# Score products on all 128 rows, and the delta rule's 64-row products taken in turn from both halves

## The chip, the cores and the metric

The kernel runs on one core of a Trainium2 chip. The metric is the device time of one execution, in microseconds (us); lower is better. The core's engines work beside each other, each through its own queue in order: TensorE (PE in the profile; PEld is its loading of stationary operands), VectorE (DVE), ScalarE (ACT), GpSimd (POOL) and the sync engine (SP), which issues the DMAs.

## The reference, cut to what matters

Four layers over one sequence of 512 positions with width 1024, in float32: an even layer (a gated recurrence and gated linear attention), an odd layer (attention with a decay), and two hybrid layers, each followed by a dense block. The change touches three things. In the odd layer, 16 heads of 64 columns:

```
s = q @ k.T                       # 512 x 512 for each head, by blocks of 128 queries
s = s + f_cum[t] - f_cum[s]       # decay, then the causal mask
o = softmax(s) @ v
```

In a hybrid layer, the same kind of scores for 4 heads with a window of 128 keys (two heads share keys) and for 4 heads with two sets of keys each, and a gated delta rule for 4 heads of 128 columns, in 8 chunks of 64 positions:

```
v_new = u_c - w_c @ state
o_c   = qd_c @ state + qk_c @ v_new
state = state * gl_c + kd_c.T @ v_new
```

## The kernel before

**Precision.** A float32 operand is split in two parts: a high part, rounded to a shorter float32 form (fp32r in the profile), and a low part, which is the rest. A projection's tile is the sum of three products in one accumulator (`mm3`, lines 590 to 592). `nc.tensor.matmul` loads its stationary operand (`lhsT`) and streams the moving one (`rhs`); each call issues its own load. Products on plain float32 operands (the transposes, the delta rule) take two passes for a call.

**Scores.** `scores` (line 1333) makes one block of 128 queries for one head. `stack` (line 1354) puts the high part of a head's 64 rows of q on one half of a 128-row tile and the low part on the other half. For k, the high part stands on both halves, so that the first product (line 1340, 128 rows) adds high by high and low by high; the second (line 1341, 64 rows of the half that holds q's high part) adds high by low. A product is at least 256 columns wide. Then VectorE adds the mask and takes the maximum (line 1349) and ScalarE the exponential (line 1351). `weigh` transposes the block (line 1371), `values` multiplies it with v (line 1385: 128 rows, 64 columns of the array, heads in turn on the two halves of the columns). `attend` (line 1388) runs these as three steps: at step t, the scores of unit t, the transposes of unit t - 3, the values of unit t - 5. Projections, gates and output products are called between units at listed steps.

In `fox` (the odd layer), `prepare` splits the operands of a pair of heads: four copies of k's high part on ScalarE (line 1503) and two low parts on GpSimd (line 1504), and two stacked q's; it is called at the fifth of the eight units of the pair before (`PREP`). The units of 8 pairs make 64 scores. `first_half`, at the eight steps of `FOX_O`, runs one tile of the first half of the output product each (`out_steps`, whose `add_gated` multiplies by a gate on VectorE, line 700, and adds to x on GpSimd, line 701); at the first of them `fetch_x` issues all eight loads of x on the sync queue. In `hybrid`, `prep_a` does the splitting for the windowed heads (low parts on VectorE, line 1717), `pair_a` and `pair_b` make 16 and 32 scores; `pair_b`'s keys stand on both halves in high and low part already.

**Delta rule.** `gdn_head` (line 1997) is a generator of about 30 steps; `skew` runs four of them, each 12 steps behind the one before, with projections called between. Its chunks lie by twos in a 128-row tile: an even chunk on rows 0 to 63, an odd one on 64 to 127. `invert16` solves 16-row blocks by many small VectorE steps and holds two accumulators meanwhile. Then lines 2118 to 2124 make a 128x128 matrix for each of six chunks: a 64-row product and a VectorE combination in turn, in the order 1, 3, 5, 2, 4, 6. The scan (lines 2126 to 2133) does, per chunk, a 64-row product (line 2129) and, on its sum, a 128-row product with the state before (line 2131), and copies the state out (line 2132). Last, lines 2135 to 2140 make the output: a 128-row product for each tile of two chunks, each followed by its two 64-column products with the states.

**Order.** The scheduler of the tile framework keeps each engine's queue about in the program's order, and lets later instructions pass those that it expects to wait. There are eight accumulators (one bank each): three for projections (`psm`), five for all else (`ps`). Work tiles are 43 slots, handed out first in, first out (`_Slots`); a slot's new user waits for its last.

Of the kernel before, what the change touches and what calls it, by code (L numbers as in the profile page):

```python
# [12 lines left out]
F32 = mybir.dt.float32  # L13
# [315 lines left out]
class _Kernel:  # L329
# [682 lines left out]
    def keep_x(self, i):  # L1012

        for h, (c, n) in enumerate(HALVES):
            self.nc.sync.dma_start(self.xkeep[i, :, c:c + n], self.x[i][h])

    def fetch_x(self, src=None, scale=None):
        src = self.xkeep if src is None else src
        for i in range(NT):
            self.x[i] = self.f(2)  # L1020
            for h, (c, n) in enumerate(HALVES):
                self.nc.sync.dma_start(self.x[i][h], src(i)[:, c:c + n] if callable(src) else src[i, :, c:c + n])
                if scale is not None:
                    (self.nc.gpsimd.tensor_scalar(self.x[i][h], self.x[i][h], scale, None, op0=OP.mult) if FXS else self.nc.scalar.activation(self.x[i][h], self.x[i][h], AF.Copy, scale=scale))
# [308 lines left out]
    def scores(self, q, k, n, bias, scale, first=None):  # L1333


        nc = self.nc
        ps = self.ps()
        if isinstance(q, tuple):
            w = max(n, 256)
            nc.tensor.matmul(ps[:, :w], lhsT=q[0], rhs=k[0], start=True, stop=False)  # L1340
            nc.tensor.matmul(ps[:, :w], lhsT=q[1], rhs=k[1], start=False, stop=True)  # L1341
        else:
            nc.tensor.matmul(ps[:, :n], lhsT=q, rhs=k, start=True, stop=True)
        s = self.f()
# [9 lines left out]
    def stack(self, t, b, at, eng):  # L1354

        d = self.slots.take(R32)
        src, hi, lo = t[b:b + 64], d[at:at + 64], d[64 - at:128 - at]
        self.nc.scalar.activation(hi, src, AF.Copy)
        eng.tensor_tensor(lo, src, hi.bitcast(F32), op=OP.subtract)
        return d  # L1360

    def scale(self, s, n, r):
# [56 lines left out]
    def fox(self, gate, done):  # L1419
# [71 lines left out]
        def pair(p):  # L1491
# [3 lines left out]
            def prepare():  # L1495
                q, k = qT.pop(p), kT.pop(p)
                st["q"] = [self.stack(q, hh * 64, hh * 64, nc.gpsimd) for hh in range(2)]
                st["k"] = [self.slots.take(R32) for _ in range(2)]
                lo = st["l"] = self.slots.take(R32)
                for hh, d in enumerate(st["k"]):  # L1500
                    b = slice(hh * 64, hh * 64 + 64)
                    for o in (hh * 64, 64 - hh * 64):
                        nc.scalar.activation(d[o:o + 64], k[b], AF.Copy)
                    nc.gpsimd.tensor_tensor(lo[b], k[b], d[b].bitcast(F32), op=OP.subtract)
                self.free(q, k)
# [12 lines left out]
            def score(i, hh):  # L1518
                def f():
# [4 lines left out]
                    n = i * 128 + 128  # L1524
                    b = slice(hh * 64, hh * 64 + 64)
                    fb, fd = st[hh]
# [3 lines left out]
                    w = max(n, 256)  # L1530
                    q, k, lo = st["q"][hh], st["k"][hh], st["l"]
                    s, m, l, r = self.scores((q[:, SL[i]], q[b, SL[i]]), (k[:, :w], lo[b, :w]), n, bias, 1.0)
                    v.reciprocal(r, l)
                    self.scale(s, n, r)
                    if i == NT - 1:
                        self.free(fb, fd)
                        if hh:
                            self.free(st["q"], st["k"], st["l"])
                    return s
# [27 lines left out]
        def first_half(t):  # L1567
            if not off:
                self.fetch_x()
                off.append(self.out_steps("od_out", 0, 0, 4, lambda k: mix[k], gate))  # L1570
            next(off[0])
            if t == FOX_O[-1]:
# [32 lines left out]
    def hybrid(self, l, gate, done):  # L1605
# [99 lines left out]
        def prep_a(p):  # L1705
            b = p * 64
            if not p:
                for h in range(2):
                    d = self.slots.take(R32)
                    ka.append(d)  # L1710
                    for o in (64 * h, 64 - 64 * h):
                        nc.scalar.activation(d[o:o + 64], ak[h * 64:h * 64 + 64], AF.Copy)
                d = self.slots.take(R32)
                ka.append(d)
                for h in range(2):
                    q = slice(h * 64, h * 64 + 64)
                    (nc.gpsimd, v)[STK[3]].tensor_tensor(d[q], ak[q], ka[h][q].bitcast(F32), op=OP.subtract)
                self.free(ak)
# [14 lines left out]
        def pair_a(p):  # L1733
            st = {}

            def score(i, hh):
                def f():
                    if i == 0 and hh == 0:
                        st["o"] = self.ps()
                    b = slice(p * 64, p * 64 + 64)  # L1740
                    j0 = max(0, i - 1)
                    n = (i + 1 - j0) * 128
                    x = p * 8 + i * 2 + hh
                    c = slice(j0 * 128, j0 * 128 + 256)
                    q = qa[p][hh]
                    s, m, ll, r = self.scores((q[:, SL[i]], q[b, SL[i]]), (ka[p][:, c], ka[2][b, c]), n, [(slice(0, n), band[:, 256 - n:])], 0.125, nsink[:, x:x + 1])
                    nc.scalar.activation(r, m, AF.Exp, bias=smt[:, 32 + x:33 + x])
# [3 lines left out]
                    if i == NT - 1 and hh:  # L1751
                        self.free(qa[p], ka[p], ka[2] if p else ())
                    return s
# [15 lines left out]
        def pair_b(p):  # L1769
            st = {}  # L1770

            def score(i, g, hh):
                def f():
                    if i == 0 and g == 1 and hh == 0:
                        st["o"] = self.ps()
                    n = i * 128 + 128
                    b = slice(hh * 64, hh * 64 + 64)
                    w = max(n, 256)
                    q, (kh, kl) = qb[p][hh], kb[g - 1]
                    s, m, ll, r = self.scores((q[:, SL[i]], q[b, SL[i]]), (kh[:, :w], kl[b, :w]), n, [(slice(0, n), cm[:, 512 - n:])], 0.125)  # L1780
                    v.reciprocal(r, ll)
# [215 lines left out]
    def gdn_head(self, h, g, xs, outs):  # L1997
# [119 lines left out]
        yield  # L2117
        for n in (1, 3, 5, 2, 4, 6):
            i, c0 = n // 2, (n % 2) * 64
            if n < 3:  # L2120
                ps = self.ps()
            q = ps[:, SL[(n - 1) // 2]]
            mm(q, lhsT=tw[c0:c0 + 64, SL[i]], rhs=kd[c0:c0 + 64, SL[i]], start=True, stop=True)  # L2123
            v.scalar_tensor_tensor(mt[n], self.ident, gl[:, n:n + 1], q, op0=OP.mult, op1=OP.subtract)
        yield
        for n in range(7):
            i, c0 = n // 2, (n % 2) * 64
            ps = self.ps()
            mm(ps[:, :128], lhsT=kd[c0:c0 + 64, SL[i]], rhs=tu[c0:c0 + 64, SL[i]], start=True, stop=n == 0)  # L2129
            if n:  # L2130
                mm(ps[:, :128], lhsT=mt[n], rhs=ss[n - 1], start=False, stop=True)
            v.tensor_copy(ss[n], ps[:, :128])
            yield
        po = self.ps()
        for i in range(NT):
            mm(po[:, SL[i]], lhsT=dt[:, SL[i]], rhs=tu[:, SL[i]], start=True, stop=False, skip_group_check=True)
            for n in (2 * i, 2 * i + 1):
                if n:
                    c0 = (n % 2) * 64
                    mm(po[c0:c0 + 64, SL[i]], lhsT=qd[:, n * 64:n * 64 + 64], rhs=ss[n - 1], start=False, stop=True, skip_group_check=True)  # L2140
        yield
# [106 lines left out]
```

## Time and profile before

| | us |
|---|---|
| Median of 3 runs | 2871.63 (2868.56 to 2872.33) |
| The profiled execution | 2869.14 |
| its span, first to last instruction | 2867.4 |
| PE busy | 2766.4 (96%) |
| DVE busy | 1972.8 (69%) |
| ACT busy | 1143.1 (40%) |
| POOL busy | 673.8 (23%) |

Engines work beside each other, so their busy times don't add up to the span. The lines of the scores have their first and last records between 720 and 2461 us; the odd layer's attention lies at about 715 to 985 us, the delta-rule stages at 1435 to 1580 and 2190 to 2340, the hybrid attentions behind each, to 1730 and 2490. The chain of waits follows back, from the last instruction, what released each step or what stood before it on its engine; the time that it shows for a product is what that product adds to the chain, which is less than its duration, since products overlap. "x4" behind a piece counts the passes merged in it.

### The profile page before, as it was taken

To read this page: it belongs to the slowest core of one execution; us is meant where nothing else is said; L and a number is where in the kernel's file an instruction comes from. 1 tells how busy PE (TensorE), PEld (TensorE's weight loads), DVE (VectorE), ACT (ScalarE), POOL (GpSimd) and SP (SyncE) were. 2 spreads that over 40 slices of the span, in tenths; PEclk is the share of its full clock that TensorE was granted. 3 is DMA by queue.
4 is the path that set the end of the run, shared out by engine and by line. 5 is a ranking of instruction groups with operands and counts; after the bars stand their busy time and mean duration, and the time that the engine had idled before them with its cause. 6 is when DMAs were issued, how large, how long until landed. Compare 5 with 4: busy or idle time off the path is not lost.

```text
span 2867.4 us, 38053 instructions
## 1 busy us (share of the span) xinstructions
PE 2766.4 (96%) x13780; PEld 2193.2 (76%) x13780; DVE 1972.8 (69%) x4170; ACT 1143.1 (40%) x2195; POOL 673.8 (23%) x530
## 2 busy tenths in 40 slices
PE   7999999998999989999999999999999999999998
PEld 5768788876666868887887668888888766788887
DVE  8978756665557776667888777666579878764445
ACT  3825233353555523324433444223254235433221
POOL 1042522435324262224011211100300112101112
PEclk9999999999999999999999999999999999999999
DMA  8635455422112355552222314554332131243322
GB/s 293 213 108 184 160 179 179 153 96 96 45 55 78 97 182 191 198 184 95 96 66 62 109 36 153 180 190 177 133 110 76 52 109 46 74 142 108 96 94 76
DMA packets 114332, 356.22 MB, mean 124 GB/s; under 512 B 13520, under 2 KB 14560, under 8 KB 114144
## 3 DMA queue, kind: packets, MB, share of 16 engines
q1 hardware_dynamic: 114144, 353.80, 36.9%
q8 instruction: 108, 1.77, 0.3%
q14 instruction: 80, 0.66, 0.1%
HBM read 341.16 MB, written 8.39 MB: 122 GB/s over the span
## 4 chain that ended last, share of the span: by engine, by line
PE 74%; DVE 8%; issue 2%; ACT 2%; POOL 1%; DMA 1%; DVEq 0%; SPq 0%; POOLq 0%; ACTq 0%
PE mm L590 20%; PE mm L591 20%; PE mm L592 20%; PE w L1385 2%; DVE wlo L597 2%; PE w L1371 2%; PE w L1341 2%; PE w L1340 1%; PE w L1009 1%; DMA adaw<-in_ada_r_dram 1%; ACT whi L596 1%; PE w L2129 1%; DVE f L762 1%; PE w L2105 1%; PE w L2123 1%
## 5 line engine op out<-in xcount | busy, mean ns | idle before, releaser
L596 ACT ACTIVATE whi<-raw 128x512 fp32r<-128x512 f32 (+1 forms) x798 | 488.4, 624 | 933.6 <-PE mm L591 436.0
L597 DVE TENSOR_TENSOR wlo<-raw,whi 128x512 fp32r<-128x512 f32 (+1 forms) x764 | 587.1, 789 | 239.9 <-ACT whi L596 225.6
L590 PE MATMUL mm<-uh,whi 128*128 128x512 f32 (+2 forms) x1896 | 720.3, 380 | 8.5 <-ACT uh L596 3.8
L591 PE MATMUL mm<-ul,whi 128*128 128x512 f32 (+2 forms) x1896 | 716.0, 378 | 1.0 <-DVE ul L597 0.7
L592 PE MATMUL mm<-uh,wlo 128*128 128x512 f32 (+2 forms) x1896 | 715.0, 377 | 0.0
L590 PE MATMUL mm<-whi,f 128*128 128x512 f32 x1120 | 449.7, 402 | 3.1 <-ACT f L596 3.1
L591 PE MATMUL mm<-wlo,f 128*128 128x512 f32 x1120 | 445.2, 398 | 0.7 <-DVE wlo L597 0.7
L592 PE MATMUL mm<-whi,f 128*128 128x512 f32 x1120 | 445.4, 398 | 0.5 <-DVE f L597 0.5
L590 PEld LDWEIGHTS mm<-uh,whi 128*128 128x128 f32 (+1 forms) x1896 | 357.6, 189 | 78.9 <-ACT uh L596 5.0
L591 PEld LDWEIGHTS mm<-ul,whi 128*128 128x128 f32 (+1 forms) x1896 | 357.2, 188 | 69.3 <-issue 3.3
L592 PEld LDWEIGHTS mm<-uh,wlo 128*128 128x128 f32 (+1 forms) x1896 | 357.4, 188 | 67.4 <-issue 2.3
L701 POOL TENSOR_TENSOR f<-f,f 128x512 f32<-128x512 f32 x144 | 203.2, 1414 | 860.3 <-DVE f L700 795.9
L590 PEld LDWEIGHTS mm<-whi,f 128*128 128x128 f32 x1120 | 212.0, 189 | 56.9 <-issue 4.9
L592 PEld LDWEIGHTS mm<-whi,f 128*128 128x128 f32 x1120 | 211.5, 189 | 52.6 <-issue 2.1
L591 PEld LDWEIGHTS mm<-wlo,f 128*128 128x128 f32 x1120 | 211.7, 189 | 50.3 <-issue 1.7
L700 DVE TENSOR_TENSOR f<-mm,gate 128x512 f32<-128x512 f32 x144 | 98.6, 686 | 205.4 <-PE mm L592 205.1
L597 DVE TENSOR_TENSOR f<-f,f 128x512 fp32r<-128x512 f32 x148 | 111.4, 758 | 75.5 <-ACT f L596 72.4
L731 DVE CUSTOM_DVE_ANT_0 adaw<-adaw,sr,colt 128x1024 f32<-128x1024 f32 x112 | 148.3, 1324 | 12.7 <-DMA adaw<-in_ada_c_dram 12.7
L596 ACT ACTIVATE f<-f 128x512 fp32r<-128x512 f32 x148 | 93.2, 631 | 144.2 <-POOL f L948 91.5
L948 POOL TENSOR_TENSOR f<-f 128x512 f32<-128x512 f32 x64 | 75.6, 1181 | 231.1 <-ACT f L947 226.7
L1351 ACT ACTIVATE f<-f,ml 128x256 f32<-128x256 f32 (+3 forms) x160 | 86.6, 541 | 77.5 <-DVE ml L1349 76.9
L547 POOL TENSOR_TENSOR raw<-raw,gate 128x512 f32<-128x512 f32 x64 | 90.0, 1431 | 85.9 <-DMA raw<-in_wd_dram 27.7
(420 smaller groups left out, 3742.3 us busy)
## 6 DMA issues: line engine op xcount, KB each, us to landing
raw<-in_w_dram SPq DMA_DIRECT2D x128, 512.0 KB, 3.7
adaw<-in_ada_c_dram SPq DMA_DIRECT2D x112, 512.0 KB, 4.5
raw<-in_wg_dram SPq DMA_DIRECT2D x88, 512.0 KB, 3.7
adaw<-in_ada_r_dram SPq DMA_DIRECT2D x64, 512.0 KB, 4.6
raw<-in_wd_dram SPq DMA_DIRECT2D x44, 512.0 KB, 3.6
raw<-in_od_qkv_dram SPq DMA_DIRECT2D x24, 512.0 KB, 3.7
raw<-in_hg_dram SPq DMA_DIRECT2D x24, 512.0 KB, 3.5
f<-in_rows_dram SPq DMA_DIRECT2D x42, 256.0 KB, 4.3
```

The costliest lines, as they stand in the source:

```text
L547: nc.gpsimd.tensor_tensor(src, src, self.open[:, half * S:half * S + S], op=OP.mult)
L590: mm(out, lhsT=a[0], rhs=b[0], start=first, stop=False)
L591: mm(out, lhsT=a[0], rhs=b[1], start=False, stop=False)
L592: self.mark = mm(out, lhsT=a[1], rhs=b[0], start=False, stop=last)
L596: self.nc.scalar.activation(hi, src, AF.Copy)
L597: (eng or self.nc.vector).tensor_tensor(lo, src, hi.bitcast(F32), op=OP.subtract)
L700: self.nc.vector.tensor_tensor(t, ps, gate[:, HALVES[h][0]:HALVES[h][0] + S], op=OP.mult)
L701: (eng or self.nc.vector).tensor_tensor(x, t, x, op=OP.add)
L731: self.nc.vector.tensor_tensor_reduce(w, w, self.sr[:, c:c + n], 0.5, at, OP.mult, OP.add, out)
L948: nc.gpsimd.tensor_tensor(t, t, t, op=OP.mult)
L1341: nc.tensor.matmul(ps[:, :w], lhsT=q[1], rhs=k[1], start=False, stop=True)
L1351: nc.scalar.activation(s[:, :n], s[:, :n], AF.Exp, bias=m, scale=-1.0, accum_out=l)
```

## The change

`scores` gets q's stacked tile and two key tiles, high and low, each on both halves, and makes both products on 128 rows with the same stationary tile; the second adds high by low and low by low. A new helper, `twice`, makes such a pair of tiles from one half: two copies and two subtractions, where there were two and one. `fox` and `prep_a` call it; a pair of heads then holds four key tiles instead of three. In `fox`, x is loaded by `fetch_half`: two of the eight parts at the first step of `FOX_O`, and one at each later step for the step after. In the delta rule, the six 64-row products stand ahead of the six combinations, in the order 1 to 6, in two accumulators by chunk parity; the scan's seven 64-row products stand together ahead of it, in two accumulators by parity, which the scan's own products then add to; and the four 128-row output products stand ahead of the seven 64-column ones.

```diff
+    def fetch_half(self, n):
+        if n == 0:
+            self.x = [[None, None] for _ in range(NT)]
+        if n < 2 * NT:
+            h, i = divmod(n, NT)
+            c, m = HALVES[h]
+            x = self.x[i][h] = self.f()
+            self.nc.sync.dma_start(x, self.xkeep[i, :, c:c + m])
...
     def scores(self, q, k, n, bias, scale, first=None):
-        if isinstance(q, tuple):
-            w = max(n, 256)
-            nc.tensor.matmul(ps[:, :w], lhsT=q[0], rhs=k[0], start=True, stop=False)
-            nc.tensor.matmul(ps[:, :w], lhsT=q[1], rhs=k[1], start=False, stop=True)
-        else:
-            nc.tensor.matmul(ps[:, :n], lhsT=q, rhs=k, start=True, stop=True)
+        w = max(n, 256)
+        nc.tensor.matmul(ps[:, :w], lhsT=q, rhs=k[0], start=True, stop=False)
+        nc.tensor.matmul(ps[:, :w], lhsT=q, rhs=k[1], start=False, stop=True)
...
+    def twice(self, t, b, eng):
+        hi, lo = self.r()
+        src = t[b:b + 64]
+        for o in (b, 64 - b):
+            self.nc.scalar.activation(hi[o:o + 64], src, AF.Copy)
+        for o in (b, 64 - b):
+            eng.tensor_tensor(lo[o:o + 64], src, hi[b:b + 64].bitcast(F32), op=OP.subtract)
+        return hi, lo
...
-                st["k"] = [self.slots.take(R32) for _ in range(2)]
-                lo = st["l"] = self.slots.take(R32)
-                for hh, d in enumerate(st["k"]):
-                    b = slice(hh * 64, hh * 64 + 64)
-                    for o in (hh * 64, 64 - hh * 64):
-                        nc.scalar.activation(d[o:o + 64], k[b], AF.Copy)
-                    nc.gpsimd.tensor_tensor(lo[b], k[b], d[b].bitcast(F32), op=OP.subtract)
+                st["k"] = [self.twice(k, hh * 64, nc.gpsimd) for hh in range(2)]
...
         def first_half(t):
-            if not off:
-                self.fetch_x()
+            n = FOX_O.index(t)
+            if not n:
+                self.fetch_half(0)
                 off.append(self.out_steps("od_out", 0, 0, 4, lambda k: mix[k], gate))
+            self.fetch_half(n + 1)
             next(off[0])
...
+                ka.extend(self.twice(ak, h * 64, (nc.gpsimd, v)[STK[3]]) for h in range(2))
...
-        for n in (1, 3, 5, 2, 4, 6):
-            i, c0 = n // 2, (n % 2) * 64
-            if n < 3:
-                ps = self.ps()
-            q = ps[:, SL[(n - 1) // 2]]
-            mm(q, lhsT=tw[c0:c0 + 64, SL[i]], rhs=kd[c0:c0 + 64, SL[i]], start=True, stop=True)
-            v.scalar_tensor_tensor(mt[n], self.ident, gl[:, n:n + 1], q, op0=OP.mult, op1=OP.subtract)
+        half = lambda t, n: t[n % 2 * 64:n % 2 * 64 + 64, SL[n // 2]]
+        pm = [self.ps() for _ in range(2)]
+        for n in range(1, 7):
+            mm(pm[n % 2][:, SL[(n - 1) // 2]], lhsT=half(tw, n), rhs=half(kd, n), start=True, stop=True)
+        for n in range(1, 7):
+            v.scalar_tensor_tensor(mt[n], self.ident, gl[:, n:n + 1], pm[n % 2][:, SL[(n - 1) // 2]], op0=OP.mult, op1=OP.subtract)
         yield
+        pk = [self.ps() for _ in range(2)]
         for n in range(7):
-            i, c0 = n // 2, (n % 2) * 64
-            ps = self.ps()
-            mm(ps[:, :128], lhsT=kd[c0:c0 + 64, SL[i]], rhs=tu[c0:c0 + 64, SL[i]], start=True, stop=n == 0)
+            mm(pk[n % 2][:, SL[n // 2]], lhsT=half(kd, n), rhs=half(tu, n), start=n < 2, stop=n == 0, skip_group_check=True)
+        for n in range(7):
+            q = pk[n % 2][:, SL[n // 2]]
             if n:
-                mm(ps[:, :128], lhsT=mt[n], rhs=ss[n - 1], start=False, stop=True)
-            v.tensor_copy(ss[n], ps[:, :128])
+                mm(q, lhsT=mt[n], rhs=ss[n - 1], start=False, stop=True, skip_group_check=True)
+            v.tensor_copy(ss[n], q)
             yield
         po = self.ps()
         for i in range(NT):
-            mm(po[:, SL[i]], lhsT=dt[:, SL[i]], rhs=tu[:, SL[i]], start=True, stop=False, skip_group_check=True)
-            for n in (2 * i, 2 * i + 1):
-                if n:
-                    c0 = (n % 2) * 64
-                    mm(po[c0:c0 + 64, SL[i]], lhsT=qd[:, n * 64:n * 64 + 64], rhs=ss[n - 1], start=False, stop=True, skip_group_check=True)
+            mm(po[:, SL[i]], lhsT=dt[:, SL[i]], rhs=tu[:, SL[i]], start=i == 0, stop=False, skip_group_check=True)
+        for n in range(1, 8):
+            c0 = (n % 2) * 64
+            mm(po[c0:c0 + 64, SL[n // 2]], lhsT=qd[:, n * 64:n * 64 + 64], rhs=ss[n - 1], start=False, stop=True, skip_group_check=True)
```

`pair_a`, `pair_b` and the scores of `fox` pass the new operands.

## Rows read from the trace of the kernel before

**Rows 1.** The page: engine, busy us, share of the span, instructions.

```profile
PE 2766.4 (96%) x13780; PEld 2193.2 (76%) x13780; DVE 1972.8 (69%) x4170; ACT 1143.1 (40%) x2195; POOL 673.8 (23%) x530
```

**Rows 2.** Busy times by stage: odd attention; delta rule, hybrid attention, twice.

```profile
715.00:985.00 270.00, 263.81 (x1377) 192.16 (x1375) 175.16 (x525) 145.48 (x322) 95.70 (x72) 1.00 0.19 62
1435.00:1580.00 145.00, 142.60 (x847) 113.74 (x845) 121.60 (x357) 51.09 (x88) 18.72 (x16) 1.00 0.21 62
1580.00:1730.00 150.00, 147.72 (x832) 98.38 (x832) 112.26 (x358) 64.86 (x181) 31.61 (x28) 1.00 0.22 69
2190.00:2340.00 150.00, 147.65 (x874) 116.58 (x873) 122.81 (x360) 49.66 (x85) 17.71 (x15) 1.00 0.22 64
2340.00:2490.00 150.00, 147.80 (x829) 99.83 (x830) 114.43 (x358) 70.70 (x193) 32.72 (x27) 1.00 0.20 66
```

**Rows 3.** Chain of waits, odd attention: start us, us added, engine, tile, line.

```profile
806.34 0.18 PE w L1340
806.52 0.36 PE w L1341
806.88 0.26 PE w L1371
...
819.60 0.12 PE w L1340
819.72 0.31 PE w L1341
...
826.82 0.37 PE w L1341
827.18 0.43 PE mm L590
827.62 0.23 PE mm L591
```

**Rows 4.** Groups by line: busy us, mean ns, idle before, whom it waited for.

```profile
L1341 PEld LDWEIGHTS w<-f,f 64*128 64x128 f32 x160 | 29.2, 183 | 31.6 <-issue 23.3
L2132 DVE COPY f<-w 128x128 f32<-128x128 f32 x56 | 16.1, 288 | 11.3 <-PE w L2131 10.2
L2124 DVE SCALAR_TENSOR_TENSOR f<-cst,ggl,w 128x128 f32<-128x128 f32 x48 | 16.0, 344 | 15.2 <-PE w L2123 15.1
```

**Rows 5.** Chain of waits, first delta-rule stage.

```profile
1494.74 0.11 PE w L1009
...
1502.31 0.36 PE w L2140 x2
1502.67 0.42 PE w L2136 x2
1503.09 0.37 PE w L2140 x4
...
1513.56 0.42 PE w L2123 x4
1513.99 0.22 PE w L2129 x2
...
1516.55 0.41 PE w L2123 x2
1516.97 0.43 PE mm L590
```

**Rows 6.** Low parts on GpSimd and VectorE; first gated sum, idle in brackets.

```profile
L1504 POOL TENSOR_TENSOR f<-f,f 64x512 fp32r<-64x512 f32 x16 | 21.2, 1326 | 24.8 <-ACT f L1503 20.7 <-PE w L1371 2.6 <-ACT f L1351 0.6
L1717 DVE TENSOR_TENSOR f<-f,f x4: 673/681/689, 1565.9 to 2321.8; 64x512 fp32r<-64x512 f32 x4
923.07 1.29 POOL L701 TENSOR_TENSOR f<-f,f 128x512 f32<-128x512 f32 x1 [2.63 <-DMA f<-xkeep]
```

**Rows 7.** Timeline of TensorE: first and last product of head 0's scan.

```profile
1474.99 0.38 PE L2129 MATMUL w<-f,f 64*128 64x128 f32 x2
1496.03 0.39 PE L2131 MATMUL w<-f,f 128*128 128x128 f32 x2
```

More of the change, by code (lines that the diff above doesn't have):

```diff
@@ L1524, in f @@
                     n = i * 128 + 128
-                    b = slice(hh * 64, hh * 64 + 64)
                     fb, fd = st[hh]
@@ L1530, in f @@
                     w = max(n, 256)
-                    q, k, lo = st["q"][hh], st["k"][hh], st["l"]
-                    s, m, l, r = self.scores((q[:, SL[i]], q[b, SL[i]]), (k[:, :w], lo[b, :w]), n, bias, 1.0)
+                    s, m, l, r = self.scores(st["q"][hh][:, SL[i]], [t[:, :w] for t in st["k"][hh]], n, bias, 1.0)
                     v.reciprocal(r, l)
@@ L1537, in f @@
                         if hh:
-                            self.free(st["q"], st["k"], st["l"])
+                            self.free(st["q"], st["k"])
                     return s
@@ L1707, in prep_a @@
             if not p:
[L1708 to L1717, printed above, removed]
+                ka.extend(self.twice(ak, h * 64, (nc.gpsimd, v)[STK[3]]) for h in range(2))
                 self.free(ak)
@@ L1739, in f @@
                         st["o"] = self.ps()
-                    b = slice(p * 64, p * 64 + 64)
                     j0 = max(0, i - 1)
@@ L1744, in f @@
                     c = slice(j0 * 128, j0 * 128 + 256)
-                    q = qa[p][hh]
-                    s, m, ll, r = self.scores((q[:, SL[i]], q[b, SL[i]]), (ka[p][:, c], ka[2][b, c]), n, [(slice(0, n), band[:, 256 - n:])], 0.125, nsink[:, x:x + 1])
+                    s, m, ll, r = self.scores(qa[p][hh][:, SL[i]], [t[:, c] for t in ka[p]], n, [(slice(0, n), band[:, 256 - n:])], 0.125, nsink[:, x:x + 1])
                     nc.scalar.activation(r, m, AF.Exp, bias=smt[:, 32 + x:33 + x])
@@ L1751, in f @@
                     if i == NT - 1 and hh:
-                        self.free(qa[p], ka[p], ka[2] if p else ())
+                        self.free(qa[p], ka[p])
                     return s
@@ L1776, in f @@
                     n = i * 128 + 128
-                    b = slice(hh * 64, hh * 64 + 64)
                     w = max(n, 256)
-                    q, (kh, kl) = qb[p][hh], kb[g - 1]
-                    s, m, ll, r = self.scores((q[:, SL[i]], q[b, SL[i]]), (kh[:, :w], kl[b, :w]), n, [(slice(0, n), cm[:, 512 - n:])], 0.125)
+                    s, m, ll, r = self.scores(qb[p][hh][:, SL[i]], [t[:, :w] for t in kb[g - 1]], n, [(slice(0, n), cm[:, 512 - n:])], 0.125)
                     v.reciprocal(r, ll)
```

## The prediction

> **What bounds the kernel now.** I read the page's busy times first, then the busy times by stage, then the chain of waits inside the stages that the change touches. TensorE (PE) is busy 2766.4 of 2867.4 us [rows 1]. In the five stages with edited lines it is as full: 263.81 of 270 us in the odd layer's attention, 142.60 of 145 and 147.65 of 150 in the two delta-rule stages, 147.72 and 147.80 of 150 in the two hybrid attentions, at a granted clock of 1.00 in all of them [rows 2]. VectorE (DVE) differs: 175.16 of 270 in the first, but 121.60 of 145 and 122.81 of 150 in the delta rule, 112.26 and 114.43 of 150 in the hybrid attentions [rows 2]. So PE's time is what the end waits for, and how much of a PE gain arrives is read from DVE.
>
> A busy PE isn't PE at its peak, so the third view matters: in the chain each product has the time that it adds. Four shapes stand there. A projection's product (512 columns, 128 rows of the array) adds 0.23 us behind one of its own shape [rows 3], a 128x128 transpose (line 1009) 0.11 [rows 5]. The scores' second product (line 1341, 64 rows of the array) behind the first one (line 1340, 128 rows): 0.31 against 0.12 at 256 columns, 0.36 against 0.18 at 384 [rows 3]. That is 0.19 more for equal columns, at each size. And what follows it pays too: the transpose behind it adds 0.26 instead of 0.11, the projection's product 0.43 instead of 0.23 [rows 3, 5]. The delta rule's rows say the same: a call (two passes) adds 0.22 us behind its own shape, 0.41 alone, and the projection behind it 0.43 [rows 5]. So each change of shape on PE (128 rows, 64 rows, 64 columns) costs 0.15 to 0.20 us of PE's own time, and the change takes such changes away. It isn't a wait for the first product's sum: three products of a projection also add into one accumulator, at 0.23 each [rows 3].
>
> **The change part by part.**
>
> **Scores.** There are 160 second products (the count of their loads [rows 4]): 64 in the odd layer (8 pairs of heads, 4 blocks, 2 heads), 48 in each hybrid layer. On 128 rows each loses its entry, 160 x 0.19 = 30.4 us. The exit depends on what follows. From 806.52 (first row) to 826.82 (last row) the chain has ten of these products: seven with transposes behind (0.15 saved), two with a projection (0.20), one with the 64-column products of line 1385, where PE changes shape anyway (nothing saved) [rows 3]. That is (7 x 0.15 + 2 x 0.20) / 10 = 0.145 us, times 160: 23.2. In sum 53.6 us of PE: 21.4 in the odd layer, 16.1 in each hybrid attention. The columns stay, and the extra term (low part times low part) adds no instruction. I count nothing for the one stationary tile: the projections' first two products share theirs too, and steps stay 0.23.
>
> The Trainium skill has a rule that speaks against this part: "TensorE: Matmul & The Clock Gate", Part 3, says that a weight load overlaps a running product only where the row group differs, so here the second load would stand open. By that page's load time (columns / 1.2, an estimate of 107 ns) 17 of the 53.6 us would go. The trace doesn't bear it out.
>
> In rows: line 1340's product of 256 columns adds 0.12 us behind another 128-row product [rows 3], though a load stands in front of each product, 0.183 us mean for line 1341's [rows 4]. So I take the loads as hidden; if not, it's a rival below.
>
> **Delta rule.** By the rows, one head costs now: six calls of line 2123, two neighbours on different halves in 0.42 and four alone at 0.41, 2.06 us; seven of line 2129, one at 0.22 and six alone, 2.68; ten exits at 0.20, 2.0; six of line 2131 at 0.22, 1.32; lines 2136 and 2140 in turn, 0.22 + 0.36 + 3 x (0.42 + 0.37), with an exit 3.15 [rows 5]. Sum 11.2. After it the calls of one shape stand together and alternate halves. Two neighbours on different halves add 0.42 with their entry of 0.19, so 0.23 a pair, half of 2 x 0.22 [rows 5]; the two halves run beside each other. Lines 2123: 0.19 + 3 x 0.23 + exit 0.20 = 1.08. Lines 2129: 0.19 + 3 x 0.23 + 0.22 + 0.20 = 1.30. Lines 2131: 1.32. Lines 2136: 0.88. Lines 2140: entry 0.14 + 3 x 0.23 + 0.22 + 0.20 = 1.25. Sum 5.8; saved 5.4 a head, 8 heads: 43 us of PE, 21.6 a layer. DVE does the same work, the six combinations now queued behind six products.
>
> **What arrives.** In the odd layer DVE would be at 175 of 249 us (70%), so 18 of 21.4. In a hybrid attention at 112 to 114 of 134 (85%): 12 of 16.1. In the delta rule a full gain leaves 123.4 us for 121.6 us of DVE work, which with its dependent chains I don't believe; I take half, 11 of 21.6. Bounds there: nothing to all. 18 + 2 x 12 + 2 x 11 = 64 us.
>
> **What it costs.** The repeated low parts. Odd layer: two more GpSimd subtractions a pair, 16 at 1.33 us mean, 21 us on an engine busy 95.70 of 270 [rows 2, 6]; behind them in its queue stand the mask sums for the next pair and the powers that release the q and k projections. They run four units ahead of use, so the attention's own products cover them; without that cover 2.7 us a pair. Hybrid: two more DVE subtractions of 0.68 us a layer [rows 6], beside projections. One more work tile is held per pair, 6 for 5; first-in-first-out slots may wait for an earlier release, or not. The eight fetches of x leave the sync queue over eight steps instead of at once: the weight loads queued behind them go earlier, each fetch later. Now the first gated sum waits 2.63 us for its fetch [rows 6]; up to that per step, eight steps, 21 us on GpSimd, none of it on PE as long as the product's accumulator is emptied by DVE before. I take 0. The scan holds two of the five accumulators where each step took one: rows show no such wait, so between a little gain (the scan's first products no longer wait for a free one) and the rival below. For all of these together I take 3 us, from -2 to +15.
>
> **Sum.** 64 - 3 = 61 us off the profiled execution's 2869.1 us (span 2867.4 and 1.7 around it): 2808. The median of the runs shown, 2871.6, lies 2.5 higher, so 2810.6.
>
> **The rivals.**
> **A. DVE binds the delta rule.** DVE is busy 84% there [rows 2], and its short dependent steps lie between PE's. Then 22 us of the 64 stay away: 2810.6 + 22 = 2833. For it: the shares; against: DVE itself stands idle now for line 2123's and 2131's products, 15.1 and 10.2 us [rows 4], which come sooner.
> **B. All of it arrives.** Products come in the order written out, and later projections fill what opens: 53.6 + 43 - 3 = 94 us, so 2778; with a few us of waits 2784.
> **C. Slower: accumulators.** The scan of head 0 runs from 1475.0 to 1496.0 us [rows 7], and the next head's 16-row inversion holds two accumulators beside it. Two and two leave one of five for every other product of both heads. If in half of a scan's 21 us both PE and DVE stood waiting, 8 x 10.5 = 84 us is lost: 2810.6 + 84 = 2895. It decides from 61 / 8 = 7.6 us a head on. Against it: projections have three accumulators of their own, and a scan whose products are ready needs the two for a shorter time. "TensorEngine Tiling (Array Packing)" of the Trainium skill, Gotcha 1, says that row tiling raises the pressure on PSUM, since row tiles write to different banks; no row here shows its price.
> **D. Loads stand open.** If the second product's load (mean 0.183 us, 160 of them [rows 4]) isn't covered, 29 us of the 53.6 go, at the share that arrives (42 of 53.6) 23 us: 2834.
> **E. It doesn't do what it says.** If the 0.19 us belongs to the second product for another reason than its rows, only the delta rule pays, with 22 us less 3: 2853.
>
> **How the numbers follow.** Forecast 0.58, A 0.16, B 0.14, C 0.04, D 0.02, E 0.03, and 0.03 for gains eaten to nothing by another order of the work. The likeliest is 2811; its own range, by the shares taken, is 2796 to 2825. The range holds the forecast, A, D and B with its few waits, leaving out C, E and the rest: 2780 to 2842. A measurement of this kernel can tell 0.2%, 5.7 us, from no change. Faster: 0.58 + 0.16 + 0.14 + 0.02 + 0.03 = 0.93; same 0.03; slower 0.04.
>
> **What would show it.** Right: the second score product adds what the first does (0.12 at 256 columns), the transpose behind it 0.11; lines 2123 and 2129 in runs of 12 and 14 passes at about 0.06 each; PE's time in the odd layer's attention down by about 20 us, DVE's share in the delta rule near 90%. Wrong, if the second product still adds 0.3; if PE waits longer for accumulators while a scan runs; if DVE's idle time in the delta rule stays at 23 to 27 us (then its chains bind, not PE); if the gated sums wait for fetches and the weights behind them. I would be most wrong in the share that arrives: nothing in the rows prices a stage in which DVE and PE are both above 90%.

## The result, and the profile after

The kernel after takes 2802.56 us (median of 4 runs, 2800.95 to 2803.64) against 2871.72 for the kernel before in the same comparison: a ratio of 0.9762 (95% interval 0.9751 to 0.9774), 69 us faster. The forecast was 2811, in a range of 2780 to 2842. The profiled execution took 2800.95 us.

**Where the time went.** I measured each stage as the time until the same number of projection products had ended in both traces, since the program orders those equally. The odd layer's attention (715 to 986 us of before) is 11.3 us shorter, the first delta rule with its attention (1435 to 1730) 28.0, the second (2190 to 2490) 28.4; all else together 0.5. The prediction had 18, 23 and 23, less 3.

The page's line of busy times and the busy times of the five stages of the kernel after (window, length, then PE, PEld, DVE, ACT and POOL busy with their instructions in brackets, granted clock, DMA share, GB/s) answer to [rows 1, 2]:

```profile
PE 2684.1 (96%) x13780; PEld 2175.2 (78%) x13780; DVE 1967.6 (70%) x4174; ACT 1141.2 (41%) x2195; POOL 704.0 (25%) x546
712.00:974.00 262.00, 250.47 (x1396) 195.37 (x1395) 180.09 (x530) 146.29 (x325) 113.52 (x84) 0.99 0.22 70
1424.00:1559.00 135.00, 131.50 (x879) 111.58 (x878) 122.97 (x368) 51.82 (x92) 19.70 (x16) 1.00 0.24 69
1559.00:1691.00 132.00, 126.99 (x799) 91.59 (x798) 105.74 (x349) 63.65 (x178) 31.59 (x28) 1.00 0.23 76
2150.00:2285.00 135.00, 131.46 (x881) 111.41 (x879) 122.46 (x367) 50.06 (x88) 18.69 (x15) 1.00 0.26 73
2285.00:2422.00 137.00, 132.50 (x825) 96.21 (x825) 110.91 (x354) 70.07 (x190) 32.91 (x27) 1.00 0.22 70
```

PE's share of the span is the same 96%; its busy time fell by 82 us and the span by 68. VectorE's work hardly moved, so it now fills 122.97 of 135 us in the first delta-rule stage, 91%, where it was 84% [rows 2]. GpSimd in the odd layer went from 95.70 to 113.52 us.

The chain of waits in the odd layer and in the delta rule (start us, us that the piece adds, engine, tile, line) answers to [rows 3, 5]. Lines 1351 and 1352 are the two score products, 1390 the transposes, 2122 and 2128 the delta rule's two groups of 64-row products, 2137 and 2140 its output:

```profile
763.09 0.17 PE w L1351
763.26 0.17 PE w L1352
763.44 0.22 PE w L1390 x2
...
889.28 0.12 PE w L1351
889.41 0.12 PE w L1352
889.53 0.23 PE mm L591
...
1519.96 0.89 PE w L2137 x8
1520.86 1.03 PE w L2140 x14
...
1531.04 0.87 PE w L2122 x12
```

The second score product adds what the first does, 0.12 at 256 columns where line 1341 added 0.31, 0.17 at 384 for 0.36; the transposes behind it add 0.11 each and a projection 0.23, for 0.26 and 0.43 [rows 3]. Line 2122 makes all six products (12 passes) in 0.87 us, where six calls alone or by twos took 2.06 by [rows 5].

Groups of instructions by line (busy us, mean ns, then the idle time before them and what ended it) answer to [rows 4, 6]; lines 2124 and 2133 are the combinations and the state's copies, 1378 the low parts:

```profile
L1352 PEld LDWEIGHTS w<-f,f 128*128 128x128 f32 x160 | 30.4, 190 | 3.4 <-issue 1.7
...
L2124 DVE SCALAR_TENSOR_TENSOR f<-cst,ggl,w 128x128 f32<-128x128 f32 x48 | 15.0, 337 | 0.1
...
L2133 DVE COPY f<-w 128x128 f32<-128x128 f32 x56 | 15.9, 284 | 7.9 <-PE w L2132 7.6
...
L1378 POOL TENSOR_TENSOR f<-f,f 64x512 fp32r<-64x512 f32 x32 | 43.9, 1371 | 29.6 <-ACT f L1376 15.1 <-DVE ml L1358 10.2 <-PE w L1390 2.3
```

VectorE no longer waits in front of the combinations: 15.2 us of idle time became 0.1. It waits 7.9 us in front of the copies, for 11.3 before.

### The profile page after: what moved, and what is told of

It reads as the page before. It is cut to its first block, busy times and chain, and to the rows that moved or that the text cites. A ratio compares the mean times of both kernels' runs of the same rounds, so it can differ in the third digit from the quotient of the medians.

```text
span 2799.2 us, 38097 instructions
## 1 busy us (share of the span) xinstructions
PE 2684.1 (96%) x13780; PEld 2175.2 (78%) x13780; DVE 1967.6 (70%) x4174; ACT 1141.2 (41%) x2195; POOL 704.0 (25%) x546
## 3 DMA queue, kind: packets, MB, share of 16 engines
q8 instruction: 108, 1.77, 0.3%
## 4 chain that ended last, share of the span: by engine, by line
PE 70%; DVE 11%; ACT 3%; issue 2%; POOL 2%; DMA 1%; DVEq 0%; POOLq 0%; SPq 0%; ACTq 0%
PE mm L592 20%; PE mm L590 20%; PE mm L591 20%; DVE wlo L597 3%; PE w L1404 2%; PE w L1390 1%; ACT whi L596 1%; PE w L1351 1%; PE w L1352 1%; DVE f L762 1%; PE w L1009 1%; DVE f L1383 1%; PE w L861 0%; DVE f L597 0%; PE w L1986 0%
## 5 line engine op out<-in xcount | busy, mean ns | idle before, releaser
L731 DVE CUSTOM_DVE_ANT_0 adaw<-adaw,sr,colt 128x1024 f32<-128x1024 f32 x112 | 145.3, 1298 | 13.8 <-DMA adaw<-in_ada_c_dram 13.5
```

What stands on the lines that cost most here:

```text
L731: self.nc.vector.tensor_tensor_reduce(w, w, self.sr[:, c:c + n], 0.5, at, OP.mult, OP.add, out)
```

## The experiments

The stages are measured as above, each against the profile of the kernel before. An edit is shown against the kernel it starts from.

**Each half of the change alone.** `e1_scores` is the kernel after with the last part of the diff (lines 2118 to 2140 of after) undone; `e2_delta` is the kernel before with that part alone.

> The change with the delta rule put back as it was: both score products on 128 rows, repeated low parts, x fetched in eight steps (with x fetched at once the work tiles don't suffice). Theory (each change of shape on PE costs 0.15 to 0.20 us, and DVE lets most of it arrive in attention): the odd layer gives 11 us as in the changed kernel, the hybrid attentions 12 each: 2871.7 - 35 = 2837, between 2832 and 2843. Rival A (DVE binds the delta rule, so that nearly all of the 69 us came from the scores): 2810 to 2820. Rival E (the 0.19 us is not the shape's): no gain, 2868 to 2880.

> The kernel before with the delta rule's new order alone. Theory (PE's time for one head falls from 11.2 to 5.8 us, and DVE, which itself waited for these products, takes most of it): the rest of the 69 us, 32 to 36: 2836 to 2840. Rival A (DVE binds): 10 us or less, 2860 to 2870. Rival C (two accumulators held through the scan starve the other heads): above 2872.

`e2_delta`: 2834.6 us (2832.26 to 2839.76), ratio 0.9873 (0.9857 to 0.9890), 36 us under the kernel before beside it (2870.52) and a little below the range that I expected. The two hybrid layers gain 17.0 and 16.9 us, the odd layer nothing. Its delta-rule stage, in the columns of the stages above, and the group of its combinations:

```profile
1434.00:1569.00 135.00, 131.33 (x878) 111.40 (x877) 121.49 (x364) 51.27 (x91) 18.99 (x16) 1.00 0.26 75
```

```profile
L2124 DVE SCALAR_TENSOR_TENSOR f<-cst,ggl,w 128x128 f32<-128x128 f32 x48 | 15.1, 339 | 0.1
```

VectorE is busy 121.49 of 135 us and the gain came all the same. So VectorE's share was no bound yet: the work stayed and the waits in front of it went.

`e1_scores`: 2843.77 us (2835.67 to 2846.86), ratio 0.9898 (0.9877 to 0.9919), just above the expected range. The odd layer gains 11.4, as in the full change, but the hybrid layers only 6.6 and 6.4. The profile says why: TensorE's clock. At the end of each delta rule it falls for 17.1 us, from 1575.7 and from 2319.8. Windows of the first of them, and a piece of its chain:

```profile
1570.00:1580.00 10.00, 9.23 (x53) 6.83 (x51) 6.28 (x16) 1.54 (x3) 0.25 (x1) 0.78 0.21 63
1580.00:1585.00 5.00, 5.00 (x16) 2.98 (x16) 0.58 (x2) 0.00 (x0) 0.00 (x0) 0.50 0.25 87
1585.00:1590.00 5.00, 5.00 (x15) 3.28 (x15) 2.55 (x8) 1.90 (x5) 0.00 (x0) 0.50 0.21 59
1590.00:1595.00 5.00, 5.00 (x31) 3.69 (x33) 3.29 (x11) 1.66 (x4) 1.01 (x1) 0.73 0.29 98
```

```profile
1578.33 0.43 PE w L2136 x2
1578.75 0.62 PE w L2140 x2
1579.37 0.73 PE w L2136 x2
```

At a granted clock of 0.50 (1.2 of 2.4 GHz) 17.1 us do the work of about 8.5. With the clock of the other traces these layers would have gained some 15 us each, an estimate. The four executions differ in the same way: 2846.86 and 2846.41 us at mean granted clocks of 0.982 and 0.983, 2841.13 at 0.986, 2835.67 at 0.988.

**Is it the shape?** `e9_both64` is the kernel before with both score products on 64 rows; q's low part by k's high part is left out. Its calls pass that half of k's high part as `k[2]`.

```diff
-            nc.tensor.matmul(ps[:, :w], lhsT=q[0], rhs=k[0], start=True, stop=False)
+            nc.tensor.matmul(ps[:, :w], lhsT=q[1], rhs=k[2], start=True, stop=False)
...
```

> The kernel before, with both score products on 64 rows of the same half (the first one reads the high half of q and k alone; the low part of q times the high part of k is left out). Theory (the 0.19 us belongs to the change of rows, not to being second in an accumulator or to the load): the second product adds 0.12 at 256 columns and 0.18 at 384 behind the first, the first one carries the 0.31 and 0.36, what follows the second still pays 0.15 to 0.20; the count of changes is that of before, so the time is too, 2866 to 2875 us. Rival (the second product is dear for another reason than its rows): the second still adds 0.31, the first 0.12, and the time is about that of before as well.

Its chain in the odd layer (lines as in the kernel before: 1340 and 1341 the two products, 1371 the transposes):

```profile
758.26 0.31 PE w L1340
758.58 0.12 PE w L1341
758.69 0.43 PE mm L592
...
764.34 0.37 PE w L1340
764.71 0.17 PE w L1341
764.88 0.26 PE w L1371
```

The 0.31 and 0.37 have moved to the first product, the second adds 0.12 and 0.17, and what follows still pays 0.43 and 0.26. The price belongs to the change of rows and to neither product. The kernel's single run took 2856.98 us, 13.5 less than before beside it, outside what I expected. Part of this has a reason in the trace: where two units' scores stand next to each other the change between them falls away too. In the odd layer there are 209 changes for 224, in the first hybrid layer 279 for 295; the three layers gain 2.3, 3.7 and 5.1 us.

**The fetch and the accumulators.** `e3_fetch` is the kernel before with the diff's `fetch_half` and its calls alone; `e6_hold` is the kernel after with a third accumulator held through each head's scan:

```diff
+        hold = self.ps()
+        mm(hold[:, :16], lhsT=mt[1], rhs=mt[1][:, :16], start=True, stop=True)
...
+        v.tensor_copy(ss[7][:, :16], hold[:, :16])
```

> The kernel before with x fetched in eight steps alone. Theory (GpSimd waits for some of the fetches, PE for none): within 4 us of 2871.7. Rival (weight loads queued behind the eight fetches were late, and this is a hidden part of the 69 us): 5 to 10 us faster. Second rival (each gated sum now waits for its fetch, and work tiles come free later): 5 to 15 us slower.

> The changed kernel with one more of the five accumulators held through each scan (a 16-column product into it ahead of the scan, a copy out of it behind: some 0.5 us a head of added work). Theory (accumulators held by the scan cost nothing that counts): 2802 to 2806. Rival C (held accumulators starve the other heads): 2810 to 2830, with PE stopping longer in the delta-rule stages.

`e3_fetch`: 2869.83 us, ratio 0.9996 (0.9985 to 1.0006): nothing, as counted. `e6_hold`: 2804.72 us, ratio 0.9771 (0.9754 to 0.9787), 2 us over the kernel after, with intervals that overlap. Even three of five accumulators held leave enough. Quite free it may not be: in its profile the two hybrid layers gain 27.3 and 24.5 us, for 28.0 and 28.4, with its own added work in that and one more fall of the clock (at 2232.6).

**The odd layer's missing 7 us.** Four kernels ask what became of them. `e4_low_dve` is the kernel after with the odd layer's low parts on VectorE. `e10_no_low` makes no low part of k there: the second product reads the high tile again. `e13_split_pool` moves half of the low parts of the odd layer's weights from VectorE to GpSimd. `e8_low_act` lets ScalarE write the repeat, as a copy of the first.

```diff
-                st["k"] = [self.twice(k, hh * 64, nc.gpsimd) for hh in range(2)]
+                st["k"] = [self.twice(k, hh * 64, v) for hh in range(2)]
```

> The changed kernel with the odd layer's low parts of k on DVE instead of GpSimd (32 subtractions, 0.68 us each on DVE against 1.3). Theory (the odd layer gave only 11 of the 18 us that I had, because the repeated low parts on GpSimd stand in the chain between two pairs of heads): 6 to 10 us faster than 2802.6, so 2793 to 2797, and PE's stops in the odd layer back from 17.6 to some 8 us. Rival (DVE's load or another order of the work took it): 2800 to 2812.

```diff
-                st["k"] = [self.twice(k, hh * 64, nc.gpsimd) for hh in range(2)]
+                st["k"] = [(self.slots.take(R32),) for hh in range(2)]
+                for hh in range(2):
+                    for o in (hh * 64, 64 - hh * 64):
+                        nc.scalar.activation(st["k"][hh][0][o:o + 64], k[hh * 64:hh * 64 + 64], AF.Copy)
...
-        [t[:, :w] for t in st["k"][hh]]
+        [t[:, :w] for t in st["k"][hh] * 2]
```

> The changed kernel without any low part of k in the odd layer: the second score product reads the high tile again, so the output lacks high by low there; PE's work is the same, GpSimd loses 32 subtractions of 1.3 us. If the repeated low parts hold the odd layer at 11 us: 2793 to 2797. If what holds it are the two chains from the q and k projections' sums (square, reduction, GpSimd's power, and five weight splits of DVE in between) and the lower clock behind PE's stops there: 2799 to 2804.

```diff
-POOL = {'ev_x': (1, 3, 4, 7)}
+POOL = {'ev_x': (1, 3, 4, 7), 'od_qkv': (1, 3, 5, 7)}
```

> The changed kernel with half of the low parts of the odd layer's q, k and v weights on GpSimd instead of DVE. If DVE's runs of five weight splits, which stand between the power and the product with it, make PE stop in the odd layer: PE's stops of 2.1 and 3.7 us shrink and its clock stays at 1.00 there, 2794 to 2799. If GpSimd, slower for each of them, becomes the late one: 2803 to 2812.

```diff
-        for o in (b, 64 - b):
-            eng.tensor_tensor(lo[o:o + 64], src, hi[b:b + 64].bitcast(F32), op=OP.subtract)
+        eng.tensor_tensor(lo[b:b + 64], src, hi[b:b + 64].bitcast(F32), op=OP.subtract)
+        self.nc.scalar.activation(lo[64 - b:128 - b], lo[b:b + 64].bitcast(F32), AF.Copy)
```

> The kernel after, with the repeat of each low part written by ScalarE, as a copy of the first, in place of a second subtraction on GpSimd (odd layer: 16 subtractions of 1.27 us less there) or VectorE. Theory (GpSimd's queue holds back the odd layer: without any low part of k that layer gained 5.7 us more): half of GpSimd's added work goes, so 2 to 5 us more in the odd layer, 2798 to 2801 us. Rival (the queue only hands the stop on, as it did when the subtractions went to VectorE): 2802 to 2804, the odd layer at 11 us gained.

Measured, with the kernel after run again beside the last one as `e15_after`:

| | us | ratio (95%) | odd layer, us | us at a clock of 0.50 there |
|---|---|---|---|---|
| after | 2802.56 | 0.9762 (0.9751 to 0.9774) | -11.3 | 6.8 |
| `e15_after`, the same kernel again | 2803.59 | 0.9765 (0.9749 to 0.9782) | -9.5 | 13.7 |
| `e4_low_dve` | 2802.82 | 0.9760 (0.9746 to 0.9775) | -11.3 | 6.8 |
| `e10_no_low` | 2797.93 | 0.9750 (0.9735 to 0.9764) | -17.0 | 3.4 |
| `e8_low_act` | 2800.01 | 0.9752 (0.9736 to 0.9768) | -14.3 | 3.4 |
| `e13_split_pool` | 2808.69 | 0.9787 (0.9772 to 0.9802) | -9.2 | 10.2 |

The last column is how long TensorE's clock stood at its lower level in that layer's attention, in the profiled execution; in the kernel before it never did. Three more kernels have the odd layer of the kernel after unchanged: `e1_scores` gains 11.4 us there, with 6.8 at the lower clock, `e6_hold` and `e5_no_alternate` (below) 12.2 each, with 3.4.

The odd-layer window of `e10_no_low`, then that of `e8_low_act`, in the columns of the stages above:

```profile
712.00:974.00 262.00, 254.05 (x1431) 199.27 (x1430) 172.56 (x535) 150.28 (x332) 79.96 (x60) 0.99 0.23 73
```

```profile
712.00:974.00 262.00, 252.90 (x1406) 196.89 (x1404) 174.70 (x531) 154.90 (x340) 96.14 (x72) 0.99 0.22 72
```

Without any low part of k the odd layer gains 17.0 us, 5.7 more than the kernel after: that is the price of making them, part of it by the clock (last section). Against `e6_hold` and `e5_no_alternate`, with as much time at the lower clock, it is 4.8. In time the kernel came out between the two ranges that I had set: the low parts hold most of the missing gain, not all. With the repeats on ScalarE GpSimd falls from 113.52 to 96.14 us and the odd layer gains 14.3. On VectorE the same subtractions cost as much as on GpSimd, where I had expected 6 to 10 us from the move; the stops only lie elsewhere. `e13_split_pool` was to shorten VectorE's five low parts in a row (shown in the next section) and made the kernel slower. It loses 5.8 us already in the stage ahead of the odd layer's attention (600 to 715), where the others of the table lose 0.3 to 2.3. The whole-kernel intervals of `e8_low_act` and of the kernel after overlap; it is the stage that speaks for it. Without the edit it gains 9.5 to 12.2 us in the five traces of the same odd layer, with it 14.3 and, in `e14_low_act_grouped` below, 14.4; at equal time at the lower clock the difference is some 2 us.

**The order of the halves.** `e5_no_alternate` is the kernel after with the 64-row and 64-column products grouped by half; `e14_low_act_grouped` does the same to `e8_low_act`.

```diff
-        for n in range(1, 7):
+        for n in (1, 3, 5, 2, 4, 6):
...
-        for n in range(7):
+        for n in (0, 2, 4, 6, 1, 3, 5):
...
-        for n in range(1, 8):
+        for n in (1, 3, 5, 7, 2, 4, 6):
```

> The changed kernel with the delta rule's products still standing together, but all of one half before those of the other (1, 3, 5, 2, 4, 6 and so on), so that neighbours share a half. Theory (two neighbours on different halves run beside each other, 0.23 us a pair against 0.44): 9 pairs lose 0.21 in all but one place of each group, about 6 pairs a head, 8 heads, 10 us of PE, of which three quarters arrive: 2808 to 2812. Rival (only the shape changes count, and DVE's load hides the rest): 2802 to 2804.

> The one before with the delta rule's 64-row products grouped by half instead of in turn. Theory (the order of the halves is worth some 4 us of TensorE in all, which VectorE's share of 91% there hides, and the 5 us by which the grouped kernel was faster were scatter): the same as the one before within 2 us. Rival (grouping is faster by itself): 4 to 5 us faster than the one before, 2793 to 2796 us.

> The kernel after unchanged, on the same chip as the two before it, for the comparison: 2800 to 2805 us. If the grouped order is no faster by itself, the grouped kernel's 2797.6 us is met by neither, and this one repeats its 2802.6 us.

`e5_no_alternate` took 2797.57 us (2796.31 to 2798.60), ratio 0.9747 (0.9732 to 0.9761); `e14_low_act_grouped` 2797.08 (2794.11 to 2801.46), ratio 0.9747 (0.9732 to 0.9763). I had expected the first to be slower than the kernel after; that fell. Of the second I then expected no more than `e8_low_act` within 2 us. It came out 2.9 us faster in the median, with runs that overlap, between the two ranges that I had set: not settled.

From 1340 to 2490 us of before, the six kernels with halves in turn and nothing else held (after, `e15_after`, `e4`, `e8`, `e10`, `e13`) gain 54.4 to 56.6 us in their profiles, the two grouped ones 59.3 and 60.8. But part of this lies where no line was edited. In the stages of the delta rule and the hybrid attention alone the six gain 55.5 to 56.9 us, the grouped ones 57.2 and 58.5. The rest is in 1340 to 1435 and 1730 to 2190: there the clock of the kernel after falls at 1395.8 and again at 2085.3, in no grouped trace at either place, and its products lose 1.8 and 1.5 us in those places. `e4_low_dve`, in turn and without the first of these falls, doesn't lose the 1.8.

One reason for what is left is in the view of who waits before line 2128's products (us, times; the longest wait of each), of the kernel after and then of `e5_no_alternate`:

```profile
  DVE f L2113: 3.2, 8
```

```profile
  DVE f L1612: 0.7, 2
```

Line 2113 empties an accumulator that line 2128 then takes. In turn, the second call already needs the second accumulator, and stands until it is free, 3.2 us in all; grouped, the first four calls go to one accumulator and the second is free by the time it is needed. Against it stands what alternation saves. TensorE has 121 changes for 127 in each hybrid layer. How much of the 5 us in the medians is the order's own isn't told apart from the clock.

## Why the prediction was right, and where its steps were off

**What bounds the kernel, and the price of a change of shape: right.** The steps came out at 0.12 and 0.17 as told, and `e9_both64` moves the price to the first product with the rows. Rival E falls. Adding up over the odd layer's trace what each product behind another shape adds above its own, I get about 38 us in 224 changes before and 17 in 104 after: some 21 us, the term of the scores. In each hybrid layer it is about 51 to 21, in 295 and 127 changes.

**The loads: right.** Line 1352's 160 loads take 190 ns each and its products add 0.12 behind a product of the same rows, so the load stays hidden. That is where "TensorE: Matmul & The Clock Gate" of the Trainium skill, Part 3, spoke against the change; these rows decide against it, and rival D falls.

**What arrives, delta rule: mis-sized.** I took 11 of 21.6 us a layer, since I didn't believe VectorE above 90%. It measured 17.0 alone (`e2_delta`), at 90%. The step that failed was to read a busy share as a ceiling: 15.1 us of VectorE's idle time stood in front of products that came sooner [rows 4], as I had noted against rival A and then not priced. Rival A falls. Nor were all of the 21.6 there. A hybrid layer of `e2_delta` has 211 changes for 295, and what they add falls by about 16 us; passes side by side save some 3 more (last section). So about 19 us of TensorE's time went, of which 17.0 arrived. In the kernel after, the scan's copies still wait 7.9 us in the two layers, and line 2128's products 3.2.

**What arrives, hybrid attention: right in size.** The whole change gains 28.0 and 28.4 a layer, the delta rule alone 17.0, so the scores add 11 behind it; 12 were taken. Alone (`e1_scores`) they gain 6.5, with the lower clock inside.

**What arrives, odd layer: the step that failed is the cover of the low parts.** I took 18 of 21.4 and, as cost, nothing for the 16 more GpSimd subtractions, "so the attention's own products cover them". It gained 11.3. In the same tally TensorE's stops (all that a product adds above the usual for its neighbour, what it loses by a lower clock included) rose by about 10 us, and 21 less 10 is the 11 that is left. `e10_no_low` prices the low parts at 5.7 us, 4.8 at an equal clock; with it the layer gains 17.0, near the 18. Of the 5.7, 1.9 lie between 860 and 900 us of before and 3.6, the clock included, between 790 and 810. The chain of the kernel after shows the first place (line 1368 is q's low part, 547 the scaling of output weights):

```profile
876.61 1.27 POOL f L1368
...
877.95 1.27 POOL f L1378
...
879.28 1.28 POOL f L1378
...
880.65 3.03 POOL raw L547 x2
...
883.75 1.28 POOL f L1378
...
885.09 1.31 POOL f L1378
...
888.76 0.52 PE w L1390 x3
```

GpSimd works 9.8 us without a break while TensorE stops three times, 2.4 us together: in its queue the low parts and the weights' scaling stand one behind the other. Before the longest of the three stops, VectorE's mask step (line 1358) stood 2.26 us until the last low part ended at 886.40, and the score product, until 887.94, for that step. The cover had been named (the products of four units) but not measured against the new length of the queue.

Two chains of small steps stop TensorE besides. They make the root mean square of a q or k (lines 1476 to 1480) and five low parts of weights on VectorE (597). Behind the first, at 744 to 753 us, it stands as long as before the change, 1.9 us in all. The second is the other place where the low parts of k cost. Its piece in the chain of the kernel after, then in that of `e10_no_low`:

```profile
789.63 5.27 DVE wlo L597 x5
```

```profile
793.17 3.09 DVE wlo L597 x5
```

The work is the same. In the kernel after two of the five ran beside low parts of k on GpSimd; the groups of that stretch (791.6 to 794.0 us):

```profile
L597 DVE TENSOR_TENSOR wlo<-raw,whi 128x512 fp32r<-128x512 f32 x2 | 3.5, 1772 | 0.0
L1378 POOL TENSOR_TENSOR f<-f,f 64x512 fp32r<-64x512 f32 x2 | 3.0, 1502 | 2.4 <-PE w L1390 2.3
```

They took 1.77 us each; the other three, with little or nothing beside them, 0.68, as all five do in `e10_no_low`. In the kernel before one ran beside a low part, and the five took 4.17 us. TensorE then stands idle for 1.93 us before, 3.33 after, 2.23 in `e8_low_act` (one again beside a low part) and 1.22 without low parts. So the cover failed twice: the longer queue came late itself, and it slowed VectorE's work in a chain that TensorE waits for. The prediction priced the subtractions by GpSimd's time alone.

**The costs, apart from that: right.** The fetch is nothing (`e3_fetch`; the gated sums of the kernel after wait 3.5 us for it in all, 2.6 before), the accumulators nothing near rival C (`e6_hold` holds a third one and loses 2 us, with intervals that overlap). They aren't wholly free: the 3.2 us before line 2128 is a wait for one. "TensorEngine Tiling (Array Packing)" of the Trainium skill, Gotcha 1, told of such pressure without a price; here it is 1.6 us a layer, and the order of the products sets it.

**The sum.** 64 less 3 was 61; the profiles give 68, as 11.3 for 18 in the odd layer, twice 28 for twice 23, and no cost beside. Two errors of opposite sign, -7 and +10, with the cost of 3 counted in the wrong place: that the sum came within 8 us is partly luck. Rival B's 94 us stays far: TensorE's busy time fell by 82 us, and not all of that arrives.

**The best version.** The repeat on ScalarE with the halves grouped gives 2797.08 us, and grouping alone 2797.57: some 5 us below the kernel after in the median. Their intervals overlap with its own and with each other, and in the profiles part of the difference is the clock.

## What to carry to other kernels

Cost a product by what it adds behind its neighbour, not by its own duration: equal columns added 0.12 or 0.31 us by the shape in front, so products of one shape belong together, and more rows can cost less than fewer. A second engine at 84% isn't a ceiling while its idle time stands in front of the very products that will come sooner; look at what ends its idle time. When the bounding engine gets faster, list the other queues that its work had covered and measure each against the shorter cover, and against what it slows beside it: here an added 18 us on an engine that was 35% busy took some 5 of 21.

## What the runs showed of the hardware that I had not expected

**VectorE's low parts take longer beside some of GpSimd's work.** In the kernel after, 714 low parts of 128x512 on VectorE (line 597) ran with GpSimd idle: the median took 0.69 us, the longest 0.70. Nine ran for most of their time beside line 1378 on GpSimd: the median took 1.76 us. Beside GpSimd's power (line 1480, 8 columns) seven took the usual 0.68. The kernel before has the same: 721 alone at 0.69, 79 beside line 701 at a median of 1.25.

**The clock falls in the odd layer where it didn't before the change.** TensorE's granted clock in the odd layer of the kernel before is 1.00 from 750 to 765 and from 795 to 805 us. The kernel after, in the windows behind the two chains, and its chain behind the second:

```profile
755.00:760.00 5.00, 5.00 (x29) 3.90 (x27) 3.57 (x13) 3.22 (x9) 4.71 (x5) 0.75 0.43 143
795.00:800.00 5.00, 1.67 (x6) 1.13 (x5) 4.98 (x13) 3.73 (x7) 3.48 (x3) 0.84 0.53 182
```

```profile
799.15 0.43 PE mm L590
799.58 0.43 PE mm L591
...
802.52 0.23 PE mm L590
```

TensorE had stood for 3.3 of the 5 us to 800, and for 1.9 before the first of these falls; the six projection products behind the second stop add 0.43 each and are then back at 0.23, though all have one shape. By the clocks of the windows 750 to 760 and 795 to 805 (0.91, 0.75, 0.84, 0.82, of 5 us each) at most 3.4 us of work are lost there. Not all of it reaches the end: `e5_no_alternate` and `e6_hold`, with the second fall alone, gain 0.9 us more in this layer. None of the four traces without the change to the odd layer (before, `e2_delta`, `e3_fetch`, `e9_both64`) shows a fall in this layer's attention; each of the ten with it spends 3.4 to 13.7 us there at the lower clock.

**It also stays low where the trace shows TensorE full.** In `e1_scores` PE is busy 5.00 of 5 us at 0.50, through the end of the delta rule in which 64-column and 128-row products take turns. In the 150 us to 1574 PE was busy 147.01 at a clock of 1.00; just before the fall, from 1570 to 1575.6, it was 4.83 of 5.60. The delta rule of after, which does the same work with fewer changes, doesn't fall there, nor does that of before, which has the same lines as `e1_scores`. In the kernel after the clock falls at 2085.3 with PE busy 5.00 of 5 us to 2090, and in the kernel before not at that place. What sets it off isn't settled by these runs. At that clock a change of shape costs 0.30 us (0.73 for a projection's product behind one, 0.43 behind its own shape) for 0.20 at the full clock.

**Two halves side by side save TensorE time, and the end doesn't show it.** Passes on opposite halves add 0.11 us a pair, on one half 0.11 each. Line 2122's 12 passes add 0.87 us in turn and 1.19 grouped, eight times; line 2128's 14, where no stop is among them, 0.89 and 1.22, and line 2140's 14 1.02 and 1.29, six times each: some 6 us in the whole kernel. The two grouped kernels give these up, and none of their nine runs was slower than the median of the kernel after.
